# A bidirectional RWKV-7 layer on one core: a new issue order for the chunked delta rule, with work moved between VectorE, GpSimd and ScalarE

## The chip, the cores and the metric

The kernel runs on one core of a Trainium2 chip. The metric is the time of one execution on the device, in microseconds. The kernel before was timed in three runs. A profile was taken of one execution; its span is the time from the first to the last instruction.

The core has five engines that run side by side, each working through its own list of instructions in the order in which the program issued them: TensorE (PE, matrix products; PEld is its loading of weights), VectorE (DVE), ScalarE (ACT), GpSimd (POOL) and SyncE (SP), which here does nothing but start DMA transfers. An instruction that has to wait for another engine or for a transfer holds up all that stands behind it on its own engine.

## The reference

One layer is computed for two sequences, 4096 and 512 tokens of width 1024: RMS norm, an input projection of which most columns are mixed with their neighbours in time, 16 heads of a delta rule with 64 x 64 states that is run forward and backward in time, a group norm, a gate, an output projection, a residual add and a final RMS norm. The part that matters here is the recurrence:

```python
def step(s, inp):
    r_t, w_t, k_t, v_t, kk_t, a_t = inp
    sa = jnp.einsum("bhvk,bhk->bhv", s, -kk_t)
    s = (s * w_t[:, :, None, :]
         + sa[..., None] * (kk_t * a_t)[:, :, None, :]
         + v_t[..., None] * k_t[:, :, None, :])
    return s, jnp.einsum("bhvk,bhk->bhv", s, r_t)
...
y_fwd = delta_rule_scan(r_h, heads(decay[:, :, 0]), heads(k_dir[:, :, 0]), v_h, kk, heads(a[:, :, 0]))
y_bwd = flip(delta_rule_scan(flip(r_h), flip(heads(decay[:, :, 1])), ...))
y = y_fwd + y_bwd
```

The decay and the mixing rate `a` of each token come from small products of rank 64 with a tanh and a sigmoid.

## The kernel before

There are three phases. The first does the norm and the input projection and leaves `r`, `k`, `v`, the normed keys and the gates in DRAM. The third does the group norm, the gate and the output projection. The change touches only the second, which does the recurrence.

**Tiling.** The second phase works on 72 blocks: 4 groups of four heads times 18 stretches of 256 tokens, 16 of them of the long sequence and 2 of the short one. A block D does both directions d (0 forward, 1 backward) and two halves hf (two heads each), and each half has four chunks i of 64 tokens. In a chunk the recurrence is replaced by products of 64 x 64 matrices, for which a unit triangular matrix is inverted for every head, direction and chunk.

**The operations of a block.** Each has a short name in the table `ISSUE`; where it ends in digits these are the half and the chunk (or part).
- SyncE: `lt`, `lk`, `lb`, `lr` load the low-rank activations, `k`, the normed keys and `r` (`load_ta` L549, `load` L541); `uv` loads `v` (L780). `ga` writes the diagonal 32 x 32 parts of the masked scores to DRAM (`gather`, L712), `gb` and `gw` read them back as `lt` and `w`, one matrix per partition (L723, L731). `S1` and `S2` write the inverse out to DRAM and read it back into `xt` (L751, L762). `yo` stores the output.
- `stage_a` (L556): `lw`, `la` are products on TensorE; `tw`, `tW`, `ta`, `tA`, `pl`, `e1`, `e2`, `fc`, `fC` are on ScalarE; `sn` (a running sum), `bf`, `bF`, `al`, `aL`, `kf`, `kF`, `rh`, `rH`, `en`, `kb`, `kk`, `kK` are on VectorE. Then `s0` to `s7` are products of scores on TensorE, `m0` to `m3` mask them on VectorE into `sc`, `x0` and `x1` transpose on TensorE, `c0` and `c1` copy on ScalarE.
- `elim` (L739): `E0` to `E14` are 15 parts of two elimination steps each on GpSimd. A step is a product into `tm` and an add into `w`, each of which needs the one before. Ones are then set on the diagonal, at the head of `S1`.
- `stage_b` (L790): `xr` transposes the pulled-in inverse on VectorE; `g0`, `g1`, `h0`, `h1` are products on TensorE and `gc`, `gC`, `hc`, `hC` copies on ScalarE that fill in the 64 x 64 inverse.
- `chain` (L841), for each half and chunk, in the order in which the data flow: `a` and `r` (TensorE, into one PSUM tile), `q` (ScalarE, copy to `rs`), `u` (TensorE, product with the inverse), `v`, `V` (ScalarE, copy to `uv`), `z` (TensorE, the new part of the state), `w`, `W` (VectorE, into the state `sn`), which the next chunk's `r` needs. `p` and `P` (`decay`, L869) write the decayed old state for direction 0 (on VectorE) and direction 1 (on ScalarE). `y` (TensorE) and `Y`, `Z` (ScalarE) give the output.

**What sets the order.** The order is written out by hand. Operation n of block D gets the position D * PERIOD + ISSUE[n], with PERIOD 27.706; all operations of all blocks are sorted by it and issued in that order (L530). Positions have no unit and don't say when an operation runs; only the order counts. Since a block's positions go from -2.9 to 146.6, five or six blocks are under way at a time. For an operation of block D at position v, v modulo 27.706 is its place in the period and v divided by 27.706 is how many blocks it lags.

**Buffers.** `k2` and `uv` have two and three buffers, `kb`, `r2`, `ta` and the tile of `bk` one, `lt` and `w` two; `xt` is one of two fixed tiles. A PSUM tile `px` is shared by `x`, `g` and `h`, another (`pl`) by the low-rank products. `BURST` adds some products at the beginning and in the last three blocks that keep TensorE busy; it isn't changed.

Of the kernel before, what the change touches and what calls it, by code (L numbers as in the profile page):

```python
# [23 lines left out]
ISSUE = {  # L24
# [44 lines left out]
def kernel(  # L69
# [62 lines left out]
    with ExitStack() as p1:  # L132
# [98 lines left out]
        # slots: one product of a column tile with a third of a token block. Each slot has small products  # L231
        # (put amid the large one) and work of the other engines, both queued by the slots before.
# [233 lines left out]
    with ExitStack() as p2:  # L466
# [89 lines left out]
        def stage_a(D, hf):  # L556
# [3 lines left out]

            def lora(x):
                z = ps.tile([128, 2, 256], F32, tag="pl", name="z")
                E["z", x] = z
                for d in range(2):
                    for n, w in enumerate(wa_q[D // NQ]):
                        PE.matmul(z[:, d, :], w[:, d, x, hf, :], S["ta"][:, d, x, :], start=(n == 0), stop=(n == 1))  # L566

            def tanh(x, d):
                n = ("qw", "qa")[x]
                if d == 0:  # L570
                    E[n] = epool.tile([128, 2, 256], F32, tag=n, name=n)
                q = E[n][:, 0, :] if d == 0 else E[n][:, 1, ::-1]
                ACT.activation(q, E["z", x][:, d, :], AF.Tanh, scale=(0.5, -0.5)[x], bias=(w0v, a0v)[x][d][:, p:p + 1])  # L573
# [29 lines left out]
            def alpha(d):  # L603
                if d == 0:
                    S["ar", hf] = d3.tile([128, 2, 4, 128], F32, tag="ar", name="ar")
                    S["tb", hf] = d3.tile([128, 2, 4, 128], F32, tag="tb", name="tb")
                    S["sc", hf] = d3.tile([128, 2, 2, 4, 128], F32, tag="sc", name="sc")
                k2 = S["k2", hf].rearrange("p d (i t) -> p d i t", t=64)
                stt(S["ar", hf][:, d, :, 0:64], k2[:, 0] if d == 0 else k2[:, 1, ::-1, ::-1], kkv[:, p:p + 1],
# [6 lines left out]
            def rho(d):  # L616
                r2 = S["r2", hf].rearrange("p d (i t) -> p d i t", t=64)
                pp = E["pp"]
                if d == 0:
                    tt(DVE, S["ar", hf][:, 0, :, 64:128], r2[:, 0], pp[:, 0, :, 1:65])  # L620
                else:
                    tt(DVE, S["ar", hf][:, 1, :, 64:128], r2[:, 1, ::-1, :], pp[:, 1, :, 64:0:-1])

            def ends():
                S["pt", hf] = d3.tile([128, 2, 4], F32, tag="pt", name="pt")
                DVE.tensor_copy(out=S["pt", hf], in_=E["pp"][:, :, :, 64])
# [8 lines left out]
            def kap_k(d):  # L635
                bk = E["bk"]
# [29 lines left out]
            def tcopy(d):  # L666
                ACT.activation(S["tb", hf][:, d], E["tp", d], AF.Copy)
# [71 lines left out]
        def elim(D):  # L739
            S = st[D]  # L740

            def e_step(j):
                lt, w = S["lt"], S["w"]
                m, n = (j + 1) // 2, 31 - j
                tm = bpool.tile([128, 128], F32, tag="tm", name="tm")
                tm = tm[:, 0:m * n].rearrange("p (c t) -> p c t", t=n)
                sh = [128, m, n]
                tt(POOL, tm, lt[:, j - 1, j + 1:32].unsqueeze(1).to_broadcast(sh), w[:, 0:m, j:j + 1].to_broadcast(sh))
                tt(POOL, w[:, 0:m, j + 1:32], w[:, 0:m, j + 1:32], tm, ALU.add)

            def scatter1():  # L751
                w = S["w"]
                wf = w.rearrange("p a b -> p (a b)")
                for c in range(2):
                    POOL.memset(wf[64 * c:64 * c + 64, c:c + 511:34], 1.0)
# [323 lines left out]
```

## Time and profile before

| | |
|---|---|
| runs | 4937.08, 4940.35, 4935.35 us; median 4937.08 |
| span of the profiled execution | 4926.0 us |
| median less span, what lies around the span | 11.1 us |
| mean granted clock of TensorE | 0.952 |
| busy in the span | PE 4484.3, DVE 3474.9, ACT 2726.9, POOL 2711.4 us |

The profiled execution's own time is listed by the page as its span only; a whole execution of the same program is some 11 us longer, as the third row shows. The page names lines of the kernel as L797 and so on. Operations that go through a small helper carry the helper's line: L86 is a product or sum of two tensors, on VectorE or GpSimd, L89 is VectorE's operation with a scalar per partition. In a timeline a row gives start, duration, engine, line, operation, output and input with their shapes, and in brackets how long the engine had been idle before and what ended it. In a row of waits stand the total, how often, and the longest. In a row of stages stand the stretch, its length, the busy time with the number of instructions of PE, PEld, DVE, ACT and POOL, the granted clock, the share of the DMA engines and GB/s.

### The profile page before, as it was taken

The page shows a single profiled execution, that of the slowest core. Times are in us where ns is not written, and L with a number is a line of the kernel's source. Part 1 is how long each engine was busy: PE and PEld are TensorE (multiplying, and loading weights), DVE is VectorE, ACT ScalarE, POOL GpSimd, SP SyncE. Part 2 cuts the span into 40 slices and gives each one's busy share as a digit, 9 for nine tenths or more (in the row PEclk, how much of TensorE's full clock was granted, in tenths as well). Part 3 has the DMA queues.
Part 4 walks back from the last instruction along what each step waited for, and adds up shares of the span by engine and source line. Part 5 has one row for each costly group of instructions (what it writes and reads, how often), then busy time and mean ns, then how long its engine had stood idle before and what let it go on. Part 6 is the DMA issues. An engine that isn't in the chain of part 4 may idle for free. (4 is left out here: it accounts for less than half of the span.)

```text
span 4926.0 us, 133131 instructions
## 1 busy us (share of the span) xinstructions
PE 4484.3 (91%) x51995; PEld 3943.8 (80%) x52005; DVE 3474.9 (71%) x6182; ACT 2726.9 (55%) x6779; POOL 2711.4 (55%) x5480
## 2 busy tenths in 40 slices
PE   8999999999999998688888888889899888896999
PEld 8999999999999997577677677677777777665887
DVE  5666666656664565677777777777777777756998
ACT  5544444444454444567666666667677666663322
POOL 3333333333333332677776777767777777764553
PEclk9999999999999998899999999989999899998999
DMA  4433333433433333455565555655656555547885
GB/s 135 147 112 112 106 113 113 123 94 122 127 106 105 97 105 109 124 141 142 134 153 142 138 142 140 150 139 140 149 142 151 137 143 140 144 98 240 269 269 188
DMA packets 1278855, 687.50 MB, mean 140 GB/s; under 512 B 665232, under 2 KB 1242768, under 8 KB 1278224
## 3 DMA queue, kind: packets, MB, share of 16 engines
q1 hardware_dynamic: 1278224, 678.99, 50.1%
q8 instruction: 408, 6.68, 0.6%
q14 instruction: 223, 1.83, 0.1%
HBM read 457.50 MB, written 221.25 MB: 138 GB/s over the span
## 5 line engine op out<-in xcount | busy, mean ns | idle before, releaser
L86 POOL TENSOR_TENSOR tm<-lt,w 128x30 f32<-128x30 f32 (+7 forms) x2160 | 864.7, 400 | 521.8 <-DMA w<-gd 340.8
L227 PE MATMUL acc<-hh,wh 128*128 128x384 f32 x3264 | 1108.0, 339 | 0.0
L229 PE MATMUL acc<-hh,wl 128*128 128x384 f32 x3264 | 1096.3, 336 | 0.0
L228 PE MATMUL acc<-hl,wh 128*128 128x384 f32 x3264 | 1096.2, 336 | 0.0
L86 POOL TENSOR_TENSOR w<-w,tm 128x30 f32<-128x30 f32 (+7 forms) x2160 | 893.5, 414 | 169.3
L228 PEld LDWEIGHTS acc<-hl,wh 128*128 128x128 f32 x3264 | 617.3, 189 | 0.0
L227 PEld LDWEIGHTS acc<-hh,wh 128*128 128x128 f32 x3264 | 617.0, 189 | 0.2
L229 PEld LDWEIGHTS acc<-hh,wl 128*128 128x128 f32 x3264 | 616.1, 189 | 0.0
L86 POOL TENSOR_TENSOR s<-u 128x384 f32<-128x384 f32 (+2 forms) x312 | 271.0, 868 | 602.1 <-ACT u L452 428.2
L89 DVE SCALAR_TENSOR_TENSOR sn<-pr,pt,sn 128x128 f32<-128x128 f32 x1152 | 346.5, 340 | 266.6 <-PE pr L894 233.8
L655 PE MATMUL sp<-ar,bk 64*128 64x128 f32 x4608 | 424.9, 309 | 9.3 <-DVE bk L86 7.4
L86 DVE TENSOR_TENSOR sc<-sp,mask 128x512 f32<-128x512 f32 x576 | 385.1, 679 | 12.7 <-PE sp L655 12.6
L452 ACT ACTIVATE u<-acc 128x384 f32<-128x384 f32 x408 | 198.2, 486 | 353.3 <-PE acc L229 353.1
L655 PEld LDWEIGHTS sp<-ar,bk 64*128 64x128 f32 x4608 | 321.7, 199 | 89.6 <-issue 32.7
L885 PE MATMUL pr<-rs,xt 64*64 64x64 f32 x4608 | 262.0, 233 | 90.6 <-ACT rs L867 89.1
L888 ACT ACTIVATE uv<-pr 64x128 f32<-64x128 f32 x1152 | 310.7, 270 | 41.9 <-PE pr L885 28.9
L86 POOL TENSOR_TENSOR xl<-rk,xh 128x384 fp32r<-128x384 f32 (+1 forms) x96 | 97.4, 1015 | 428.2 <-ACT xh L259 428.2
L867 ACT ACTIVATE rs<-py 128x128 f32<-128x128 f32 x576 | 159.2, 277 | 302.7 <-PE py L863 296.4
L885 PEld LDWEIGHTS pr<-rs,xt 64*64 64x64 f32 x4608 | 182.7, 136 | 163.0 <-ACT rs L867 110.9
L566 PE MATMUL z<-ta,wah 128*128 128x256 f32 x576 | 191.8, 352 | 115.1 <-ACT qw L573 95.5
L797 DVE STREAM_TRANSPOSE x<-xt 128x512 f32<-128x512 f32 x72 | 51.2, 711 | 338.4 <-DMA xt<-wd 338.4
L86 DVE TENSOR_TENSOR xl<-kq,xh 128x384 fp32r<-128x384 f32 (+1 forms) x96 | 93.3, 972 | 269.7 <-ACT xh L259 269.7
(163 smaller groups left out, 10470.7 us busy)
## 6 DMA issues: line engine op xcount, KB each, us to landing
wr<-in_rw_in_dram SPq DMA_DIRECT2D x136, 512.0 KB, 4.3
ta<-ta_d SPq DMA_DIRECT2D x144, 256.0 KB, 2.9
k<-k_d SPq DMA_DIRECT2D x288, 128.0 KB, 2.8
r<-r_d SPq DMA_DIRECT2D x288, 128.0 KB, 2.2
kb<-kb_d SPq DMA_DIRECT2D x288, 128.0 KB, 3.4
uv<-v_d SPq DMA_DIRECT2D x288, 128.0 KB, 2.9
y_d<-ys SPq DMA_DIRECT2D x144, 256.0 KB, 3.9
lt<-gd SPq DMA_DIRECT2D x144, 240.0 KB, 3.6
```

The source lines that it names most:

```text
L86: eng.tensor_tensor(out=out, in0=a, in1=b, op=op)
L89: DVE.scalar_tensor_tensor(out=out, in0=a, scalar=s, in1=b, op0=op0, op1=op1)
L227: PE.matmul(ps, wh[:, k, :], hh[:, k, :], start=(k == 0), stop=False)
L228: PE.matmul(ps, wh[:, k, :], hl[:, k, :], start=False, stop=False)
L229: PE.matmul(ps, wl[:, k, :], hh[:, k, :], start=False, stop=(k == KT - 1))
L452: ACT.activation(u[:, 2 + s * SUB:2 + (s + 1) * SUB], ps[:, 0:SUB], AF.Copy, scale=(0.5 if typ == "g" else 1.0))
L566: PE.matmul(z[:, d, :], w[:, d, x, hf, :], S["ta"][:, d, x, :], start=(n == 0), stop=(n == 1))
L655: PE.matmul(E["sp"][h][:, d, j, :], bk_(d, i)[hs], ar[hs, d, i, :], start=True, stop=True)
L797: DVE.transpose(out=x, in_=S["xt"][:, :, 0:32])
L867: ACT.activation(S["rs", hf], rp, AF.Copy)
L885: PE.matmul(up[ua[d], hs], S["xt"][ua[d], 8 * hf + 4 * h + i, :], rs[ua[d], hs], start=True, stop=True)
L888: ACT.activation(S["uv", hf][ua[d], d, (i, 3 - i)[d], :], up[ua[d]], AF.Copy)
```

## The change

Three things change, all in the second phase.

1. Every entry of `ISSUE` has a new value, so the order of all operations changes on all five engines. PERIOD stays.
2. `E6` and `E12`, the parts 6 and 12 of the fifteen of the elimination, run on VectorE, with a temporary tile of their own (`td`). The setting of the diagonal becomes an operation of its own (`ms`), still on GpSimd.
3. `p`, the decay of the forward state, runs on ScalarE for all four chunks (`ACT_DECAY = 4`).

The rest follows from the new order: tiles that were made by one named operation are made by whichever comes first (`kept`, `tile_bk`, `state_tile`), the PSUM tiles `iv` of `g` and `h` have names of their own, and the state before a chunk is looked up by its number (`before`).

```diff
+ON_DVE = (6, 12)
+ACT_DECAY = 4
 ISSUE = {
-    "wa": -2.946, "lt": 0.000, "lk0": 2.020, "lw0": 3.600, "lr0": 5.680, "tw0": 8.955, "tW0": 9.315,
...
-    "m01": 44.495, "m11": 45.105, "x01": 45.320, "c01": 45.960, "s41": 46.412, "s61": 46.854, "x11": 48.502,
-    "s51": 48.944, "c11": 49.142, "s71": 49.386, "m21": 50.626, "m31": 52.116, "ga1": 58.442, "gb": 62.192,
-    "gw": 64.482, "E0": 68.302, "E1": 69.594, "E2": 71.070, "E3": 72.701, "E4": 74.458, "E5": 76.312,
-    "E6": 78.234, "E7": 80.196, "E8": 82.169, "E9": 84.124, "E10": 86.032, "E11": 87.864, "E12": 89.592,
-    "E13": 91.187, "E14": 92.620, "S1": 95.488, "uv0": 98.678, "S2": 99.958, "xr": 103.358, "a00": 105.682,
...
+    "wa": -2.9000, "lt": 0.0000, "lk0": 1.1591, "lw0": 1.2805, "lb0": 3.3493, "tw0": 7.3949, "tW0": 8.8003,
...
+    "e11": 26.1877, "lr1": 27.5209, "s70": 27.6598, "s60": 27.6701, "rH1": 27.7889, "al1": 27.9700,
+    "s40": 28.0035, "s50": 28.7095, "bf1": 28.7498, "e21": 28.8191, "aL1": 29.0697, "fc1": 29.1549,
+    "rh1": 30.5646, "fC1": 33.6847, "kf1": 33.7227, "en1": 33.7493, "kb1": 34.0198, "kF1": 35.3220,
...
+    "s61": 41.9178, "s71": 42.8163, "c01": 42.8473, "s41": 43.6381, "m31": 43.6723, "ga0": 44.0974,
+    "m21": 44.6119, "ga1": 45.5600, "x11": 45.7879, "c11": 46.5981, "gw": 49.6933, "gb": 50.5948, "E0": 57.5603,
+    "E1": 62.9549, "E2": 64.2336, "E3": 68.6505, "E4": 70.0206, "E5": 70.3026, "E6": 73.5289, "E7": 74.7859,
+    "E8": 76.3981, "E9": 79.0079, "E10": 82.8529, "uv0": 83.5557, "E11": 83.7589, "E12": 84.4780,
+    "E13": 87.3066, "E14": 87.5877, "ms": 88.8890, "S1": 90.1739, "S2": 94.4958, "xr": 98.0045, "g0": 102.1712,
+    "g1": 102.6785, "uv1": 103.3862, "gC": 103.6546, "gc": 104.5328, "a00": 104.7541, "p00": 107.0296,
+    "r00": 107.9962, "h0": 108.9094, "q00": 109.5492, "P00": 109.7186, "h1": 109.9664, "a10": 110.5160,
+    "hC": 110.6414, "hc": 110.6737, "r10": 111.1384, "q10": 111.3443, "P10": 111.3638, "u00": 111.3691,
+    "u10": 111.3799, "v00": 111.3876, "V00": 111.5611, "v10": 111.5624, "a11": 111.6107, "V10": 111.6683,
+    "z00": 111.6767, "a01": 111.7563, "z10": 112.1606, "W00": 112.2069, "w00": 112.4946, "r01": 112.6950,
...
+    "W13": 136.3979, "Y11": 136.5489, "w13": 136.6701, "Z11": 137.9200, "yo": 142.4142,
 }
...
+            def kept(n, *shape):
+                if (n, hf) not in S:
+                    S[n, hf] = d3.tile([128, *shape], F32, tag=n, name=n)
+                return S[n, hf]
...
+            def tile_bk():
+                if "bk" not in E:
+                    E["bk"] = bpool.tile([128, 2, 576], F32, tag="bk", name="bk")
+                return E["bk"]
...
-            def e_step(j):
+            def e_step(j, eng):
                 lt, w = S["lt"], S["w"]
                 m, n = (j + 1) // 2, 31 - j
-                tm = bpool.tile([128, 128], F32, tag="tm", name="tm")
+                n_ = "tm" if eng is POOL else "td"
+                tm = bpool.tile([128, 128], F32, tag=n_, name=n_)
                 tm = tm[:, 0:m * n].rearrange("p (c t) -> p c t", t=n)
                 sh = [128, m, n]
-                tt(POOL, tm, lt[:, j - 1, j + 1:32].unsqueeze(1).to_broadcast(sh), w[:, 0:m, j:j + 1].to_broadcast(sh))
-                tt(POOL, w[:, 0:m, j + 1:32], w[:, 0:m, j + 1:32], tm, ALU.add)
+                tt(eng, tm, lt[:, j - 1, j + 1:32].unsqueeze(1).to_broadcast(sh), w[:, 0:m, j:j + 1].to_broadcast(sh))
+                tt(eng, w[:, 0:m, j + 1:32], w[:, 0:m, j + 1:32], tm, ALU.add)
+
+            def ones():
+                wf = S["w"].rearrange("p a b -> p (a b)")
+                for c in range(2):
+                    POOL.memset(wf[64 * c:64 * c + 64, c:c + 511:34], 1.0)
...
             def e_block(b):
                 for j in range(1 + 30 * b // EB, 1 + 30 * (b + 1) // EB):
-                    e_step(j)
+                    e_step(j, DVE if b in ON_DVE else POOL)
...
+        def state_tile(hf, n):
+            if (hf, n) not in cur:
+                cur[hf, n] = spool.tile([128, 2, 128], F32, tag=f"sn{hf}", name="sn")
+            return cur[hf, n]
...
-            def first(i):
-                return i == 0 and q in FIRST
+            def before(i):
+                return zero if i == 0 and q in FIRST else cur[hf, 4 * D + i - 1]
...
             def decay(i, d):
...
+                pt, o = S["pt", hf][:, d, i:i + 1], state_tile(hf, 4 * D + i)[:, d, :]
+                if d == 0 and i >= ACT_DECAY:
+                    DVE.tensor_scalar(out=o, in0=before(i)[:, d, :], scalar1=pt, scalar2=None, op0=ALU.mult)
                 else:
-                    ACT.activation(o, cur[hf][:, d, :], AF.Copy, scale=pt)
+                    ACT.activation(o, before(i)[:, d, :], AF.Copy, scale=pt)
```

The places in the period of a few more operations that the prediction speaks of, in the new order: on TensorE r10 0.3, u00 0.5, u10 0.6, a11 0.8, z00 0.9, u01 2.8, a02 4.2, r11 5.0, z01 5.8, u11 6.1; on SyncE lt 0.0, uv0 0.4, lk0 1.2, lb0 3.3, yo 3.9, S1 7.1, S2 11.4, ga0 16.4, lk1 17.1, ga1 17.9, lr0 18.6, lb1 20.2, uv1 20.3, gw 22.0, gb 22.9, lr1 27.5. SyncE's order before was lt 0.0, lr1 1.0, lk0 2.0, ga1 3.0, lr0 5.7, gb 6.8, yo 8.1, gw 9.1, lb0 10.3, lk1 11.4, S1 12.4, ga0 13.7, uv0 15.6, S2 16.8, lb1 19.0, uv1 25.7.

More of the change, by code (lines that the diff above doesn't have):

```diff
@@ L569, in tanh @@
                 n = ("qw", "qa")[x]
-                if d == 0:
+                if n not in E:
                     E[n] = epool.tile([128, 2, 256], F32, tag=n, name=n)
@@ L594, in bfac @@
             def bfac(d):
-                if d == 0:
+                if "ah" not in E:
                     E["ah"] = epool.tile([128, 2, 256], F32, tag="qw", name="ah")
@@ L619, in rho @@
                 if d == 0:
-                    tt(DVE, S["ar", hf][:, 0, :, 64:128], r2[:, 0], pp[:, 0, :, 1:65])
+                    tt(DVE, kept("ar", 2, 4, 128)[:, 0, :, 64:128], r2[:, 0], pp[:, 0, :, 1:65])
                 else:
-                    tt(DVE, S["ar", hf][:, 1, :, 64:128], r2[:, 1, ::-1, :], pp[:, 1, :, 64:0:-1])
+                    tt(DVE, kept("ar", 2, 4, 128)[:, 1, :, 64:128], r2[:, 1, ::-1, :], pp[:, 1, :, 64:0:-1])
             def ends():
-                S["pt", hf] = d3.tile([128, 2, 4], F32, tag="pt", name="pt")
-                DVE.tensor_copy(out=S["pt", hf], in_=E["pp"][:, :, :, 64])
+                DVE.tensor_copy(out=kept("pt", 2, 4), in_=E["pp"][:, :, :, 64])
+            def tile_bk():
+                if "bk" not in E:
+                    E["bk"] = bpool.tile([128, 2, 576], F32, tag="bk", name="bk")
+                return E["bk"]
             def kap_b():
-                bk = bpool.tile([128, 2, 576], F32, tag="bk", name="bk")
-                E["bk"] = bk
+                bk = tile_bk()
                 e8 = E["ee"]
@@ L635, in kap_k @@
             def kap_k(d):
-                bk = E["bk"]
+                bk = tile_bk()
                 e8 = E["ee"]
@@ L650, in scores @@
                 ar, i = S["ar", hf], 2 * i2 + j
-                if (d, j) == (0, 0):
-                    E["sp"] = [ps.tile([128, 2, 2, 128], F32, tag=("pa", "pb")[h], name="sp") for h in range(2)]
+                if ("sp", i2) not in E:
+                    E["sp", i2] = [ps.tile([128, 2, 2, 128], F32, tag=("pa", "pb")[h], name="sp") for h in range(2)]
                 for h in range(2):
                     hs = slice(64 * h, 64 * h + 64)
-                    PE.matmul(E["sp"][h][:, d, j, :], bk_(d, i)[hs], ar[hs, d, i, :], start=True, stop=True)
+                    PE.matmul(E["sp", i2][h][:, d, j, :], bk_(d, i)[hs], ar[hs, d, i, :], start=True, stop=True)
             def masks(i2, h):
-                tt(DVE, S["sc", hf][:, :, h, 2 * i2:2 * i2 + 2, :], E["sp"][h],
+                tt(DVE, kept("sc", 2, 2, 4, 128)[:, :, h, 2 * i2:2 * i2 + 2, :], E["sp", i2][h],
                    mask.unsqueeze(2).to_broadcast([128, 2, 2, 128]))
@@ L666, in tcopy @@
             def tcopy(d):
-                ACT.activation(S["tb", hf][:, d], E["tp", d], AF.Copy)
+                ACT.activation(kept("tb", 2, 4, 128)[:, d], E["tp", d], AF.Copy)
             for n, *f in (
@@ L713, in gather @@
             S = st[D]
-            if f == 0:
+            if "gd" not in S:
                 S["gd"] = dsc.tile([2, 2, 2, 4, 2, 32, 32], F32, tag="gd", name="gd")
@@ L772, in e_block @@
                 for j in range(1 + 30 * b // EB, 1 + 30 * (b + 1) // EB):
-                    e_step(j)
+                    e_step(j, DVE if b in ON_DVE else POOL)
             for b in range(EB):
                 add(f"E{b}", D, e_block, b)
+            add("ms", D, ones)
             add("S1", D, scatter1)
@@ L799, in g_mm @@
             def g_mm(n):
-                if n == 0:
-                    S["iv"] = ps.tile([128, 16, 32], F32, tag="px", name="iv2")
-                pt = S["iv"]
+                if "iv2" not in S:
+                    S["iv2"] = ps.tile([128, 16, 32], F32, tag="px", name="iv2")
+                pt = S["iv2"]
                 for x in range(8 * n, 8 * n + 8):
@@ L810, in g_cp @@
                 q = 64 * d
-                ACT.activation(S["g"][q + 32:q + 64], S["iv"][q + 32:q + 64], AF.Copy)
+                ACT.activation(S["g"][q + 32:q + 64], S["iv2"][q + 32:q + 64], AF.Copy)
             def x_mm(n):
-                if n == 0:
-                    S["iv"] = ps.tile([128, 16, 32], F32, tag="px", name="iv3")
-                pt = S["iv"]
+                if "iv3" not in S:
+                    S["iv3"] = ps.tile([128, 16, 32], F32, tag="px", name="iv3")
+                pt = S["iv3"]
                 for x in range(8 * n, 8 * n + 8):
@@ L824, in x_cp @@
                 q = 64 * d
-                ACT.activation(S["xt"][q:q + 32, :, 32:64], S["iv"][q:q + 32], AF.Copy)
+                ACT.activation(S["xt"][q:q + 32, :, 32:64], S["iv3"][q:q + 32], AF.Copy)
             for n, *f in (
@@ L858, in step_r @@
             def step_r(i):
-                if first(i):
-                    cur[hf] = zero
-                S["old", hf, i] = cur[hf]
                 for d in range(2):
-                    PE.matmul(rp[ua[d], :], S["ar", hf][:, d, i, 0:64], cur[hf][:, d, :], start=False, stop=True)
+                    PE.matmul(rp[ua[d], :], S["ar", hf][:, d, i, 0:64], before(i)[:, d, :], start=False, stop=True)
             def copy_r(i):
@@ L869, in decay @@
             def decay(i, d):
-                if d == 0:
-                    S["sn", hf] = spool.tile([128, 2, 128], F32, tag=f"sn{hf}", name="sn")
-                if first(i):
-                    cur[hf] = zero
-                pt, o = S["pt", hf][:, d, i:i + 1], S["sn", hf][:, d, :]
-                if d == 0:
-                    DVE.tensor_scalar(out=o, in0=cur[hf][:, d, :], scalar1=pt, scalar2=None, op0=ALU.mult)
+                pt, o = S["pt", hf][:, d, i:i + 1], state_tile(hf, 4 * D + i)[:, d, :]
+                if d == 0 and i >= ACT_DECAY:
+                    DVE.tensor_scalar(out=o, in0=before(i)[:, d, :], scalar1=pt, scalar2=None, op0=ALU.mult)
                 else:
-                    ACT.activation(o, cur[hf][:, d, :], AF.Copy, scale=pt)
+                    ACT.activation(o, before(i)[:, d, :], AF.Copy, scale=pt)
             def step_u(i):
@@ L905, in step_y @@
                 for d in range(2):
-                    PE.matmul(o[d], S["ar", hf][:, d, i, 64:128], S["old", hf, i][:, d, :], start=True, stop=False)
+                    PE.matmul(o[d], S["ar", hf][:, d, i, 64:128], before(i)[:, d, :], start=True, stop=False)
                 for h in range(2):
```

13 lines of the change are left out of this document (2 added, 11 removed), and 51 rows, old and new, of the table ISSUE.

## The prediction

> **What bounds the kernel now.** Only the second phase is touched, so I first ask where it lies and how long one block of it takes. The page gives the span, the view of one tile's instructions gives the first and last VectorE transpose of the pulled-in inverse (one per block, 72 blocks), and the view by stages gives the engines' busy time between those two.
>
> ```profile
> span 4926.0 us, 133131 instructions
> L797 DVE STREAM_TRANSPOSE x<-xt x72: 711/711/714, 2036.5 to 4416.0; 128x512 f32<-128x512 f32 x72
> 2036.50:4416.00 2379.50, 2104.46 (x38417) 1689.79 (x38425) 1755.48 (x4113) 1612.02 (x4625) 1738.26 (x4381) 0.93 0.57 141
> ```
>
> 71 periods take 2379.5 us, so one block costs 33.5 us. Per block TensorE is busy 29.6 us, VectorE 24.7, ScalarE 22.7, GpSimd 24.5 (the columns are PE, weight loads, DVE, ACT, POOL). TensorE is idle 3.9 us per block, and a granted clock of 0.93 means that it ran at half speed for some 0.14 of the time, 4.7 us per block. No engine is full. So I next read who waits for whom in the same stretch (total, times, longest).
>
> ```profile
> DVE x L797 <- DMA xt<-wd: 333.2, 71, 16.4
> POOL tm L86 <- DMA w<-gd: 286.6, 65, 8.9
> ACT qw L573 <- DVE bk L86: 203.1, 66, 17.5
> PE pr L885 <- ACT rs L867: 87.4, 90, 1.3
> PE z L566 <- ACT qw L573: 80.7, 64, 1.7
> PE iv L806 <- DVE x L797: 56.5, 52, 2.2
> PE pr L894 <- ACT uv L888: 21.7, 72, 0.7
> ```
>
> VectorE stands 4.7 us in every block for the inverse to come back from DRAM, and GpSimd stands 4.0 us for the next block's matrices. Each engine works strictly in the issued order, so VectorE's stand holds up what is queued behind it: ScalarE's `qw` waits for `bk`, and TensorE waits for `qw` and `x`, (80.7 + 56.5) / 71 = 1.9 us of its 3.9 us. The rows of four microseconds show the hole and its echo (last figures: clock, DMA share, GB/s).
>
> ```profile
> 3020.00:3024.00 4.00, 3.24 (x50) 2.54 (x46) 0.31 (x1) 2.48 (x8) 3.31 (x9) 1.00 0.71 154
> 3024.00:3028.00 4.00, 2.28 (x67) 2.18 (x68) 4.00 (x9) 1.56 (x4) 3.45 (x8) 0.64 0.38 113
> 3028.00:3032.00 4.00, 4.00 (x33) 2.88 (x34) 3.96 (x9) 0.83 (x3) 3.37 (x9) 0.51 0.51 157
> ```
>
> VectorE does 0.31 us of work in 3020 to 3024, TensorE thins out, and then the granted clock is 0.64 and 0.51.
>
> Why do both stands occur in every block? The timelines of VectorE, SyncE's queue and GpSimd give the ring.
>
> ```profile
> 3023.69 0.71 DVE L797 STREAM_TRANSPOSE x<-xt 128x512 f32<-128x512 f32 x1 [4.94 <-DMA xt<-wd]
> 3027.75 0.68 DVE L86 TENSOR_TENSOR sc<-sp,mask 128x512 f32<-128x512 f32 x1
> ```
> ```profile
> 3014.43 1.26 SPq L760 DMA_DIRECT2D wd<-w  x2
> 3020.18 2.14 SPq L768 DMA_DIRECT2D xt<-wd  x4
> 3032.00 2.33 SPq L720 DMA_DIRECT2D gd<-sc  x4
> 3039.46 0.81 SPq L546 DMA_DIRECT2D r<-r_d  x2
> 3043.19 1.64 SPq L737 DMA_DIRECT2D w<-gd  x2
> ```
> ```profile
> 3004.79 0.49 POOL L86 TENSOR_TENSOR w<-w,tm 128x84 f32<-128x84 f32 x1
> 3007.11 0.61 POOL L86 TENSOR_TENSOR tm<-lt,w 128x56 f32<-128x56 f32 x1
> 3010.23 0.30 POOL L755 MEMSET w<- 64x16 f32 x2
> 3014.42 0.24 POOL L86 TENSOR_TENSOR tm<-lt,w 128x30 f32<-128x30 f32 x1 [3.90 <-DMA w<-gd]
> 3027.14 0.41 POOL L86 TENSOR_TENSOR tm<-lt,w 128x128 f32<-128x128 f32 x1
> ```
>
> Block D's elimination starts at 3014.42 and ends, memsets included, one period after 3010.53, at 3044.0: 29.6 us. Its transpose follows 13.2 us after the memsets (3010.53 to 3023.69). Behind the transpose stand masks of block D+2, done at 3028.43, 4.7 us after its start. Only then may D+2's gather go out, but SyncE issues it at 3032.00 to 3034.33 (5.9 us), then waits with a load of `r` until 3039.46, and is done with `w<-gd` at 3044.83 (10.5 us). The elimination of D+2 begins 3.1 us later, at 3014.42 + 67.0 - 33.5 = 3047.9. The pieces, 29.6 + 13.2 + 4.7 + 5.9 + 10.5 + 3.1 = 67.0 us, are exactly two periods of 33.5. This **ring over two blocks** sets the pace; TensorE does not.
>
> **The change, part by part.**
>
> *Two parts of the elimination move to VectorE.* Part 6 is the steps of 126 and 119 elements, part 12 those of 78 and 65, two instructions each: eight instructions per block. GpSimd loses 1.8 us of part 6 (from the 126 row below, 0.472 + 0.523, to the start of part 7 at 3027.14) plus the stretch from 3005.28 to 3007.11 for part 12, about 3.9 us in all. On VectorE no such instruction was run; the floor is its 8-element copy (0.300), the ceiling GpSimd's own 0.523. I take 0.33, nearest the 128-element `sn` rows: 8 x 0.33 = 2.6 us, bounds 2.4 to 4.2.
>
> ```profile
> L86 POOL TENSOR_TENSOR w<-w,tm 128x126 f32<-128x126 f32 x142 | 74.2, 523 | 11.1
> L86 POOL TENSOR_TENSOR tm<-lt,w 128x126 f32<-128x126 f32 x142 | 67.0, 472 | 11.1
> L626 DVE COPY pt<-pp 128x8 f32<-128x8 f32 x138 | 41.4, 300 | 0.0
> L876 DVE TENSOR_SCALAR sn<-sn,pt 128x128 f32<-128x128 f32 x551 | 179.2, 336 | 3.1 <-PE py L906 2.9
> L878 ACT ACTIVATE sn<-sn,pt 128x128 f32<-128x128 f32 x551 | 219.0, 398 | 1.8
> ```
>
> *The forward decay* is eight instructions per block: VectorE loses 8 x 0.336 = 2.7 us and ScalarE gains 8 x 0.398 = 3.2 us. VectorE stays at 24.7 - 2.7 + 2.6 = 24.6 us and ScalarE comes to 25.9. Both stay below what TensorE needs (next part), but ScalarE's copies are on the recurrent path of the states and now meet more company.
>
> *The queue of SyncE.* Nothing is added to it; its order changes. S1 (to `wd`) now has S2 (to `xt`) right behind it, with no loads between, and ga0, lk1, ga1, lr0, lb1, uv1, gw, gb follow. So S2 makes the queue wait for S1's landing; queued behind are the gathers, and they would wait for the masks behind the transpose anyway. I price the two hops with the landings of the page's kind of row:
>
> ```profile
> wd<-w SPq DMA_DIRECT2D x142, 128.0 KB, 2.8
> xt<-wd SPq DMA_DIRECT2D x284, 64.0 KB, 2.6
> ```
>
> S1's second issue starts 0.6 us in and lands 2.8 us later, at 3.4; S2's last of four starts 1.6 us on and lands at 3.4 + 1.6 + 2.6 = 7.6 us, in place of 13.2. The three loads now between ga1 and gw (some 0.8 to 1.3 us each by the `r` and `wd` rows) hide ga1's landing, and the wait for `r`'s buffer is gone from there: `lr0` stands at 18.64, its buffer's last readers (`rH1`, `rh1`) at 27.79 and 30.56, a period earlier relative to it.
>
> *The ring after the change.* Taking positions modulo the period of 27.706, a period reads: E0 of the next block on GpSimd at 2.1, E13, E14 and memsets from 4.2, S1 7.1, S2 11.4, transpose 14.9, last masks 16.0 and 16.9 (of the block two later), E6 on VectorE 18.1, E7 on GpSimd 19.4 through E11, E12 on VectorE at 1.4. That makes a ring of **one** period: E6 on VectorE 1.4; E7 to E11 11.6 (3027.14 to 3005.28, one period on); E12 with two engine changes 1.5, beside which E0 of the next block runs (four instructions of the size in the row of 3014.42, some 1.3 us); E13 to memsets 3.4 (3007.11 to 3010.53); hops 7.6; transpose and two masks 0.7 + 0.68 + 0.6 = 2.0. The sum is 27.5 us. The gather's ring closes over one period too, from E0 through memsets, hops, masks, ga1 (2.3), three loads (3.0), gw and gb (2.8) and a landing (3.1): 1.3 + 3.4 + 7.6 + 2.0 + 2.3 + 3.0 + 2.8 + 3.1 = 25.5 us. Both are shorter than TensorE's need, but not by much.
>
> [...]
>
> *TensorE's need.* Its work is unchanged. In the half-clock stretch one `r` product group takes 0.69 us, at full clock 0.44:
>
> ```profile
> 3007.02 0.44 PE L863 MATMUL py<-sn,ar 128*64 128x128 f32 x4
> 3030.12 0.69 PE L863 MATMUL py<-sn,ar 128*64 128x128 f32 x4
> ```
>
> So of 4.7 us at half clock 4.7 x (1 - 0.44 / 0.69) = 1.7 us was loss, and the work at full clock is 29.6 - 1.7 = **27.9 us**. To that come three things. First, the new order has places where a result cannot be back in time. The rows below give the round trips: r at 3007.02, its copy at 3007.60; copy at 3013.29, u at 3013.62; so r to u takes 0.91 us, of which r's own turn is 0.37. u at 3004.04, copies at 3004.67, z at 3005.29: 1.25 us, less u's turn of 0.38.
>
> ```profile
> 3007.60 0.28 ACT L867 ACTIVATE rs<-py 128x128 f32<-128x128 f32 x1 [0.45 <-PE py L863]
> 3013.29 0.28 ACT L867 ACTIVATE rs<-py 128x128 f32<-128x128 f32 x1
> ```
> ```profile
> 3004.04 0.45 PE L885 MATMUL pr<-rs,xt 64*64 64x64 f32 x8
> 3005.29 0.45 PE L894 MATMUL pr<-uv,tb 128*64 128x64 f32 x8
> 3013.62 0.45 PE L885 MATMUL pr<-rs,xt 64*64 64x64 f32 x8 [1.03 <-ACT rs L867]
> ```
>
> So an r wants 0.54 us of other products behind it before its u, and a u 0.87 before its z. Between r10 and u10 stands only u00 (0.38), between r11 and u11 only z01 (0.38); u01 has a02 and r11 (0.71) and u00 has u10 and a11 (0.76) before their z. These four are short by 0.16 + 0.16 + 0.16 + 0.11 = 0.6 us; the old order had every such pair covered. Second, queueing on ScalarE: today TensorE waits (87.4 + 21.7) / 71 = 1.5 us per block for copies; I scale it by ScalarE's load, 25.9 / 31 against 22.7 / 33.5, to 1.9 us. Third, some clock loss stays: I take half, 0.8 us, because the largest hole closes and small ones remain. [...]
>
> *Sum.* 27.9 + 0.6 + 1.9 + 0.8 = 31.2 us per block, 2.3 less: 71 x 2.3 = 163 us. Lead-in and tail: the first transpose moves from position 103.4 to 98.0 and the end from 43.2 behind it to 44.4, a net of 4.2 positions at 33.5 / 27.7 = 1.2 us, 5 us less. The span would be 4926 - 168 = 4758 us. The runs' median, 4937, lies 11 us above the span; I keep that, and get **4769 us**.
>
> **The rivals.** (A) *TensorE nearly full*: clock loss gone and queueing only half of today's: 27.9 + 0.6 + 0.7 = 29.2 us, which gives 4937 - 71 x 4.3 - 5 = 4627 us. For it speaks that the rings have 27.5 us; against it ScalarE's longer queue. (B) *The one-period ring becomes the pace, slower than before.* Place: VectorE at E6 and E12, where it now stands for GpSimd, with the states' updates queued behind. If the two hops still take 13.2 us (the DMA engines are already busy 0.57 of the stretch, and the new order sends its transfers in one long row), the ring is 27.5 + 5.6 = 33.1; if VectorE also comes to E6 and E12 with about one scan-sized backlog in all (1.3 us, my estimate of its queue there), 34.4 us: 4937 + 71 x 0.9 - 5 = 4996 us. It decides from a ring above 33.5, that is 6 us more than the sum above. For it: four changes of engine and two hops in one period; against it: S2 no longer has SyncE's other work ahead. (C) *The gain is eaten by short waits*: TensorE's idle time stays 3.9 us and the clock 0.93 though the stands are gone, 33.5 us per block, 4932 us. Against it: 1.9 of the 3.9 us are pinned on the stand. (D) Half of the gain only, 32.4 us: 4937 - 78 - 5 = 4854 us, if the missing cover and ScalarE's growth, which I put at 0.6 + 0.4, cost 2.2 us, as they would if each copy came a tenth of a microsecond later than today.
>
> **How the numbers follow.** Forecast 0.55, A 0.11, D 0.17, B 0.12, C 0.05. A measurement of this kernel can tell about 0.2%, 10 us, from no change. Forecast, A and D are faster: 0.83. C is the middle of no change and just faster: 0.04 for the same. B is slower: 0.13 with C's edge. The forecast's own range is 30.2 to 32.2 us per block, 4698 to 4840. The range reaches over D and most of C, and towards A to 29.7 us: 4660 to 4932, leaving out B, and the better half of A.
>
> **What would show it.** Right: the spacing of the transposes falls to about 31.2 us; the waits of VectorE for `xt` and of GpSimd for `w` fall well below 1 us per block; S1's issue to the transpose takes under 9 us; granted clock above 0.95; ScalarE's waits for TensorE shrink while TensorE's for `rs` grow. Wrong: new waits of VectorE's `td` and `w` for GpSimd, or of GpSimd's `tm` for VectorE above some 3 us per block (B); a clock still at 0.93 (C).

## The result and the profile after

The changed kernel ran in 4771.35 us (median, 4767.1 to 4778.97) beside 4936.22 us for the kernel before on the same chip: a ratio of 0.9667 with a 95% interval of 0.9653 to 0.9681. The forecast was 4769 us.

The same three rows as before the change, from the page, the view of the transpose's tile and the view by stages:

```profile
span 4772.0 us, 133366 instructions
...
L810 DVE STREAM_TRANSPOSE x<-xt x72: 697/699/714, 2028.0 to 4258.4; 128x512 f32<-128x512 f32 x72
...
2028.00:4258.40 2230.40, 1983.10 (x38351) 1580.65 (x38351) 1717.81 (x4114) 1745.80 (x5181) 1640.56 (x3818) 0.96 0.62 150
```

A block now takes 2230.4 / 71 = 31.4 us in place of 33.5. The second phase between first and last transpose gave 149.1 us, lead-in and tail (span less that stretch) 4.9 us: 2546.5 before, 2541.6 after. TensorE is idle (2230.4 - 1983.1) / 71 = 3.5 us per block, busy 27.9, and its mean clock is 0.96.

Who waits for whom in that stretch. The row of the transpose among VectorE's groups stands in for its wait (busy, mean, idle before and what ended it); the others are totals, times and longest.

```profile
L810 DVE STREAM_TRANSPOSE x<-xt 128x512 f32<-128x512 f32 x71 | 49.7, 700 | 2.1 <-DMA xt<-wd 2.1
```
```profile
POOL tm L91 <- DVE w L91: 288.2, 139, 7.4
ACT rs L882 <- PE py L878: 154.2, 175, 2.9
DVE ar L91 <- DMA r<-r_d: 123.5, 54, 5.8
PE py L915 <- ACT rs L882: 99.2, 212, 0.7
PE pr L896 <- ACT rs L882: 47.0, 70, 0.8
PE pr L905 <- ACT uv L899: 33.8, 129, 0.6
PE z L576 <- DMA ta<-ta_d: 28.1, 46, 3.8
POOL tm L91 <- DMA lt<-gd: 15.3, 19, 2.4
```

The two stands that the prediction built on are gone: VectorE's wait for `xt` fell from 333.2 us to 2.1, GpSimd's wait for the gathered matrices from 286.6 (for `w`) to 15.3 (for `lt`). New are GpSimd's waits for VectorE's two parts, 4.1 us per block, VectorE's wait for the load of `r`, 1.7, and TensorE's wait at the output product (L915) for a copy of `rs`, 1.4.

The timelines of SyncE, GpSimd and VectorE show the way round:

```profile
3004.74 1.26 SPq L772 DMA_DIRECT2D wd<-w  x2
3007.99 1.93 SPq L780 DMA_DIRECT2D xt<-wd  x4
...
3015.32 1.80 SPq L729 DMA_DIRECT2D gd<-sc  x4
...
3021.55 1.27 SPq L746 DMA_DIRECT2D w<-gd  x2
```
```profile
3004.59 0.30 POOL L764 MEMSET w<- 64x16 f32 x2
...
3016.59 0.89 POOL L91 TENSOR_TENSOR tm<-lt,w 128x128 f32<-128x128 f32 x1 [1.84 <-DVE w L91]
```
```profile
3013.42 0.70 DVE L810 STREAM_TRANSPOSE x<-xt 128x512 f32<-128x512 f32 x1
3014.05 1.25 DVE L91 TENSOR_TENSOR sc<-sp,mask 128x512 f32<-128x512 f32 x2
3015.22 0.26 DVE L91 TENSOR_TENSOR td<-lt,w 128x126 f32<-128x126 f32 x1
```

From the memsets' end at 3004.89 to the transpose are 8.5 us in place of 13.2, and the transpose doesn't wait. The gather goes out at 3015.32, as the masks end at 3015.30; before, 3.6 us passed there. `w<-gd` follows it 6.2 us later (before 11.2).

### The profile page after: what moved, and what is told of

Same layout as the page of the kernel before. It is cut to its first block, busy times and chain, and to the rows that moved or that the text cites. A ratio compares the mean times of both kernels' runs of the same rounds, so it can differ in the third digit from the quotient of the medians.

```text
span 4772.0 us, 133366 instructions
## 1 busy us (share of the span) xinstructions
PE 4369.3 (92%) x52005; PEld 3842.4 (81%) x52005; DVE 3437.4 (72%) x6182; ACT 2866.8 (60%) x7355; POOL 2608.6 (55%) x4904
## 4 chain that ended last, share of the span: by engine, by line
PE 63%; ACT 14%; DVE 7%; DMA 6%; issue 5%; POOL 2%; SPq 1%; ACTq 0%; DVEq 0%; POOLq 0%
PE acc L232 10%; PE acc L234 10%; PE acc L233 10%; PE acc L1039 8%; DMA ta<-ta_d 4%; ACT uv L899 3%; PE z L576 3%; PE py L915 3%; PE pr L896 3%; PE sp L664 3%; PE py L919 2%; PE py L878 2%; PE pr L905 2%; PE tp L673 2%; DMA r<-r_d 2%
## 5 line engine op out<-in xcount | busy, mean ns | idle before, releaser
L91 POOL TENSOR_TENSOR tm<-lt,w 128x120 f32<-128x120 f32 (+7 forms) x1872 | 818.6, 437 | 486.8 <-DVE w L91 291.1
L91 POOL TENSOR_TENSOR w<-w,tm 128x120 f32<-128x120 f32 (+7 forms) x1872 | 838.3, 448 | 146.7
L889 ACT ACTIVATE sn<-sn,pt 128x128 f32<-128x128 f32 x1120 | 436.5, 397 | 40.5 <-PE py L915 34.4
L91 DVE TENSOR_TENSOR sc<-sp,mask 128x512 f32<-128x512 f32 x576 | 372.3, 676 | 41.6 <-PE sp L664 40.7
L664 PE MATMUL sp<-ar,bk 64*128 64x128 f32 x4608 | 384.2, 296 | 8.2 <-DVE sc L91 6.4
L664 PEld LDWEIGHTS sp<-ar,bk 64*128 64x128 f32 x4608 | 302.5, 192 | 61.5 <-issue 30.6
L915 PE MATMUL py<-sn,ar 128*64 128x128 f32 x2240 | 250.6, 304 | 97.5 <-ACT rs L882 97.5
L896 PE MATMUL pr<-rs,xt 64*64 64x64 f32 x4608 | 251.3, 235 | 48.6 <-ACT rs L882 48.6
L905 PE MATMUL pr<-uv,tb 128*64 128x64 f32 x4608 | 260.1, 236 | 35.9 <-ACT uv L899 35.7
L91 DVE TENSOR_TENSOR wl<-wr,wh 128x1024 fp32r<-128x1024 f32 x136 | 182.8, 1344 | 137.0 <-ACT wh L223 136.8
```

The costliest lines, as they stand in the source:

```text
L91: eng.tensor_tensor(out=out, in0=a, in1=b, op=op)
L664: PE.matmul(E["sp", i2][h][:, d, j, :], bk_(d, i)[hs], ar[hs, d, i, :], start=True, stop=True)
L889: ACT.activation(o, before(i)[:, d, :], AF.Copy, scale=pt)
L896: PE.matmul(up[ua[d], hs], S["xt"][ua[d], 8 * hf + 4 * h + i, :], rs[ua[d], hs], start=True, stop=True)
L905: PE.matmul(zp[hs, d, hs], S["tb", hf][:, d, i, hs], S["uv", hf][:, d, (i, 3 - i)[d], hs], start=True, stop=True)
L915: PE.matmul(o[d], S["ar", hf][:, d, i, 64:128], before(i)[:, d, :], start=True, stop=False)
```

## The experiments

Each kernel was timed beside the kernel before on the same chip. Its median was 4940, 4961 and 4956 us in the three groups of runs, so the ratios are compared, not the times.

**The moves alone, in the old order.** The changed kernel's code with the old table:

```diff
-    "wa": -2.9000, "lt": 0.0000, "lk0": 1.1591, "lw0": 1.2805, "lb0": 3.3493, "tw0": 7.3949, "tW0": 8.8003,
...
+    "wa": -2.946, "lt": 0.000, "lk0": 2.020, "lw0": 3.600, "lr0": 5.680, "tw0": 8.955, "tW0": 9.315,
...
+    "E13": 91.187, "E14": 92.620, "ms": 95.487, "S1": 95.488, "uv0": 98.678, "S2": 99.958, "xr": 103.358, "a00": 105.682,
```

> The old order of all operations, with parts 6 and 12 of the elimination on VectorE and the forward decay on ScalarE (ms directly ahead of S1). Theory R (the ring over two blocks, closed by SyncE's order, sets the pace): the moves alone take 3.9 us off GpSimd in the ring and put about 2.2 us of VectorE back into it, with E6 right behind the transpose; 33 to 34.5 us per block, 4890 to 5000 us, VectorE still waits over 3 us per block for xt. Rival M (the gain is GpSimd's and VectorE's relieved load): below 4850 us.

Measured: 5004.77 us, ratio 1.0132 (1.01 to 1.0165). The waits of its second phase:

```profile
POOL tm L89 <- DVE w L89: 431.0, 142, 9.1
...
DVE x L808 <- DMA xt<-wd: 246.7, 67, 6.3
POOL tm L89 <- DMA w<-gd: 229.7, 63, 5.2
```

The old stands shrank to 3.5 and 3.2 us per block, and GpSimd got a third: 6.1 us per block for VectorE. In the old order the moves cost time. The time came out just above the range of theory R, and VectorE's wait for `xt` fits it; rival M, that the moves by themselves bring the gain, has fallen.

**The new order alone.**

```diff
-ON_DVE = (6, 12)
-ACT_DECAY = 4
+ON_DVE = ()
+ACT_DECAY = 0
```

> The new order of all operations, but all fifteen parts on GpSimd and the forward decay on VectorE as before. Theory R: most of the gain is there without the moves, 4740 to 4840 us; GpSimd then has 29.4 us of work per block, just below TensorE's pace. Rival M: above 4880 us.

Measured: 4816.93 us, ratio 0.9755 (0.9725 to 0.9785). That lies in the range of theory R: most of the gain, 2.4 of 3.3%, needs neither move.

**SyncE's queue alone, first try.** The order of the four other engines is the old one, and neither move is made; of the table, the entries that differ from the kernel before:

```diff
-    "lr0": 5.680, "lb0": 10.350, "lk1": 11.360, "ga1": 58.442, "gb": 62.192, "gw": 64.482, "S2": 99.958,
+    "lr0": 16.9, "lb0": 12.70, "lk1": 12.75, "ga1": 52.20, "gb": 54.60, "gw": 54.55, "S2": 95.60,
```

> The old order of TensorE, ScalarE, VectorE and GpSimd and no moves; in SyncE's queue alone seven operations stand elsewhere: S2 right behind S1, lb0 and lk1 behind S2, lr0 behind uv0, ga1 right behind the masks m31, gw and gb right behind uv1. Theory R: the hops fall from 13.2 to about 7.6 us and the gather's way from 16 to about 8, the ring falls below TensorE's need, VectorE's wait for xt goes below 1 us per block, 31.3 to 32.5 us per block, 4780 to 4865 us. Rival O (it is the order on the working engines that counts): above 4890 us.

Measured: 5256.5 us, ratio 1.0648 (1.0619 to 1.0676): a miss by more than 390 us. VectorE's wait for `xt` is no longer among the long ones, but these are, in the second phase:

```profile
DVE ar L89 <- DMA r<-r_d: 345.7, 68, 7.0
PE z L574 <- DMA ta<-ta_d: 331.2, 69, 6.8
POOL tm L89 <- DMA lt<-gd: 309.2, 35, 12.5
```
```profile
SPq L937 <- ACT ys L923: 450.6, 70, 11.6
SPq L727 <- DVE bk L89: 381.6, 66, 8.4
```

SyncE stood 5.4 us per block before a gather (L727), and the loads of `ta` and `r`, which I had left behind `ga1`, came late: TensorE waited 4.7 us per block for `ta`, VectorE 4.9 for `r`. The run doesn't decide between the theories, because it removed one wait and made others; it shows how much a queue's order alone can cost.

**SyncE's queue alone, second try.** Six entries, the loads of `ta` and of the second half's `r` staying ahead of `gw` and `gb`:

```diff
-    "lr0": 5.680, "ga1": 58.442, "gb": 62.192, "gw": 64.482, "S2": 99.958, "uv1": 108.818,
+    "lr0": 16.9, "ga1": 52.20, "gb": 56.52, "gw": 56.51, "S2": 95.60, "uv1": 107.568,
```

> Once more the old order with SyncE's queue alone changed, now without delaying the loads that are needed soon: S2 right behind S1; lr0 behind S2 and uv0; ga1 right behind the masks m31 with uv1 ahead of it; gw and gb behind ta's and r's loads. Theory R (the two-block ring set the pace): the hops fall from 13.2 to about 7.6 us, the way from m31 to the landing of w and lt from 19.5 to about 10, the ring to about 52 us for two blocks; VectorE's wait for xt goes below 1 us per block and the period to 31.3 to 32.8 us: 4780 to 4890 us. Rival O (the order on the working engines makes the gain; the ring was only one of several equally long): the waits go, but others take their place, 33 us or more per block, above 4900 us.

Measured: 4812.12 us, ratio 0.9696 (0.9663 to 0.9728). Tile, stage and waits:

```profile
L808 DVE STREAM_TRANSPOSE x<-xt x72: 697/699/712, 2033.7 to 4293.4; 128x512 f32<-128x512 f32 x72
...
2033.70:4293.40 2259.70, 2087.58 (x38363) 1679.06 (x38369) 1717.70 (x4113) 1602.64 (x4615) 1798.43 (x4386) 0.94 0.61 148
```
```profile
POOL tm L89 <- DMA lt<-gd: 91.1, 35, 9.5
...
DVE x L808 <- DMA xt<-wd: 13.3, 6, 10.9
```

31.8 us per block; the wait for `xt` went from 333.2 us to 13.3. Six entries in the queue of an engine that computes nothing give 3.0 of the 3.3% of the whole change, and the two intervals overlap. So the order of SyncE's queue set the pace, and rival O has fallen. Which of the six entries counts was not separated. Nor has any run the changed kernel's code with the old table and without the moves, so the rest of that code (tile names, `ms`) is counted with the six.

**The same with the forward decay on ScalarE** (`ACT_DECAY = 4` added to that table).

> The old order with SyncE's six entries moved (that alone 0.970) and the forward decay on ScalarE. If the decay's gain is a matter of VectorE's load: 0.955 to 0.963. If it depends on the new order, which puts the decays elsewhere on ScalarE: 0.968 to 0.980.

Measured: 4782.43 us, ratio 0.9637 (0.9596 to 0.9678), between the two expectations, and its interval overlaps that of the queue alone. It can't be told from the whole change, though all engines but SyncE run by the old table. Without the decay the new order gave 0.9755 and the old one with six entries 0.9696; with the decay (the new order's run is the second of the next two) they gave 0.9663 and 0.9637. No run shows a gain that the new order of the four working engines brings by itself.

**The decay and the two parts, each alone in the new order.** First the decay back on VectorE (`ACT_DECAY = 0`), the parts staying:

> The changed kernel with the forward decay back on VectorE; parts 6 and 12 stay on VectorE. VectorE gains 2.7 us per block, ScalarE loses 3.2. If the moves' 46 us (the order alone ran 4817) come from GpSimd's relief: 4760 to 4790 us. If they come from the decay, which leaves VectorE free for the states' updates: 4805 to 4840 us.

Measured: 4866.57 us, ratio 0.9809 (0.9778 to 0.9841). Then the parts back on GpSimd (`ON_DVE = ()`), the decay staying on ScalarE:

> The new order with the forward decay on ScalarE, but all fifteen parts of the elimination on GpSimd. Order alone ran at 0.9755 of before, order with the two parts at 0.981, the changed kernel at 0.967. If the decay's effect (0.986) doesn't depend on the parts: 0.959 to 0.965, faster than the changed kernel, and the two parts on VectorE cost time. If the parts pay only once VectorE is relieved of the decay: 0.970 or more.

Measured: 4787.71 us, ratio 0.9663 (0.9637 to 0.9688). So the decay is worth 0.9% without the parts (0.9755 to 0.9663) and 1.4% with them (0.9809 to 0.9667). The two parts on VectorE bring nothing once the decay is gone from it (0.9663 against 0.9667), and 0.9755 against 0.9809, with intervals that just touch, suggests that they cost something while it is there. What the decay gains shows mostly in the clock. The stretch 2036 to 4200 of the kernel with the parts and without the decay:

```profile
2036.00:4200.00 2164.00, 1909.25 (x35638) 1522.13 (x35631) 1757.87 (x4398) 1505.66 (x4322) 1481.14 (x3548) 0.92 0.61 147
```

Its transposes are 32.7 us apart, so TensorE is idle 3.9 us per block (3.5 with the decay moved) and busy 28.9 (27.9), and the clock is 0.92 in place of 0.96, which by the correction used below accounts for the 1 us of busy time. Why the clock is lower with the decay on VectorE was not traced.

**Three output products earlier.** The cause of TensorE's wait at L915 is seen in one place of the changed kernel (TensorE's and ScalarE's timelines):

```profile
3002.30 0.39 PE L878 MATMUL py<-sn,ar 128*64 128x128 f32 x4
...
3003.13 0.44 PE L915 MATMUL py<-sn,ar 128*64 128x128 f32 x4 [0.44 <-ACT rs L882]
```
```profile
3002.80 0.28 ACT L882 ACTIVATE rs<-py 128x128 f32<-128x128 f32 x1 [0.97 <-PE py L878]
```

An output product y follows an r of the same half at once and waits until ScalarE has copied that r. Both write the tile `py` in PSUM, the memory into which this kernel's products go, in different columns. It occurs 212 times, three per block: y00 behind r01, y01 behind r02, y12 behind r13. The edit moves the three y ahead of the product `a` that opens the next sum in that tile, and two of these `a` move too:

```diff
-    "y00": 113.5131, "y01": 119.3339, "a02": 115.0080, "y12": 131.8283, "a13": 129.0234,
+    "y00": 111.70, "y01": 116.64, "a02": 116.65, "y12": 129.42, "a13": 129.43,
```

> The changed kernel, with three output products moved ahead of the next chunk's first products: y00 ahead of a01, y01 and then a02 right behind z01, y12 and then a13 right behind z12. In the changed kernel these three stand directly behind r01, r02 and r13 in the same PSUM bank and TensorE waits 1.4 us per block there for the copy of r. If that wait lies on the path, 0.5 to 1.3 us per block go: 4680 to 4735 us. If another wait takes its place: 4760 to 4785 us.

Measured: 4716.69 us, ratio 0.9554 (0.9529 to 0.9579), faster than both kernels.

```profile
2029.40:4204.00 2174.60, 1941.89 (x38366) 1558.99 (x38364) 1754.54 (x4114) 1746.65 (x5182) 1572.31 (x3817) 0.98 0.64 154
```
```profile
PE pr L896 <- ACT rs L882: 113.6, 218, 0.8
```

30.6 us per block, 0.8 less. TensorE's waits for `rs` at L915, 99.2 us before the edit, are below the 6.5 us of the last row of the list, but TensorE's idle time fell only from 3.5 to 3.3 us: its wait for `rs` before u rose from 47.0 us to 113.6. The rest came from busy time, 27.9 to 27.4 us, with the clock at 0.98. So the time lies in the range that was expected if the wait was on the path, but by the correction used below 0.5 of the 0.8 us came by the clock, and only 0.2 by idle time.

**The load of r earlier.** One entry of the changed kernel:

```diff
-    "lr1": 27.5209,
+    "lr1": 21.80,
```

> The changed kernel with one entry changed: lr1, the load of r for the second half, stands ahead of gw in SyncE's queue instead of behind gb. In the changed kernel VectorE waits 1.7 us per block for it, most of it in some fifty blocks. If that wait is on the path, most of it goes: 4660 to 4730 us. If delaying gw and gb by about 1 us for it costs the elimination as much, or TensorE has other waits by then: 4755 to 4790 us.

Measured: 4886.07 us, ratio 0.9841 (0.9811 to 0.9871): a miss on both expectations. The waits of the second phase, SyncE's first:

```profile
SPq L729 <- DVE td L91: 241.4, 68, 7.9
...
SPq L551 <- DVE ar L91: 31.2, 45, 1.2
```
```profile
POOL tm L91 <- DMA lt<-gd: 77.2, 45, 4.5
PE z L576 <- DMA ta<-ta_d: 74.9, 95, 4.9
```

SyncE now waits for VectorE's last use of the one buffer of `r` (L551) with `gw`, `gb` and `ta` behind it. GpSimd's wait for `lt` rose from 15.3 us to 77.2 and TensorE's for `ta` from 28.1 to 74.9. The new wait is only 0.4 us per block, the block takes 1.3 us longer (32.7), and SyncE's stand before a gather (L729) grew more than any of these, from 150.8 us to 241.4; the whole way from the one to the other was not traced. A second buffer for `r`, which no run has, would test the wait itself, so whether VectorE's 1.7 us lie on the path isn't settled.

**Both edits together.**

> Both small edits of the order together: three output products ahead of the next chunk's first products (alone 4717 us) and lr1 ahead of gw. If they are independent: 4620 to 4690 us; if they close the same gap: 4700 to 4720 us.

Measured: 4891.35 us, ratio 0.9849 (0.9817 to 0.9882). That can't be told from the load alone (0.9841): beside it the output products bring nothing.

**Output products earlier and no parts on VectorE**, then **with part 12 only**.

> The kernel of the run before, with the three output products and two first products moved as in the run that gave 0.955. If all effects multiply: 0.945 to 0.953. If GpSimd's full 29.4 us per block now bounds: 0.955 to 0.965, with GpSimd's idle time below 1 us per block.

> The changed kernel with the five entries moved as in the run that gave 0.955, and only part 12 on VectorE, part 6 back on GpSimd. GpSimd waits for VectorE after both parts, 4.1 us per block in the changed kernel. If the wait after part 6, behind the transpose and the masks, is what costs: 0.945 to 0.952. If GpSimd's idle time is slack: 0.953 to 0.960.

Measured: 4709.41 us, ratio 0.9502 (0.9476 to 0.9527), and 4750.71 us, ratio 0.9591 (0.956 to 0.9622). The first is the fastest kernel of the study and lies in the range for effects that multiply; its interval just clears that of the same order with both parts (0.9554, 0.9529 to 0.9579). Part 12 alone can't be told from both, and is clearly slower than none: one part costs no less than two. The time lies in the range for slack in GpSimd's idle time, but then the step from no part to part 12 should cost nothing; neither account fits, and the cause stays open.

## Why the prediction was right, step by step

**The ring over two blocks: right in the queue that it named, which was tested by itself.** Six entries of SyncE's queue gave a ratio of 0.9696, and VectorE's wait for `xt` went with them. The sum of 67.0 us was no evidence, though. Its end, 3014.42 + 67.0 - 33.5, is set from the period itself, and any way from the start of one elimination to that of the next but one adds up to two periods, spare time included. What spoke for the ring were the waits at two of its links. At a third, the gather, 3.6 us passed after the masks were done at 3028.43, in which SyncE issued three loads (kernel before):

```profile
3028.55 0.89 SPq L554 DMA_DIRECT2D ta<-ta_d  x2
3030.05 0.81 SPq L546 DMA_DIRECT2D r<-r_d  x2
3031.16 0.80 SPq L546 DMA_DIRECT2D k<-k_d  x2
```

The data were there and the queue's order made the gather late; that is what the six entries changed. In the changed kernel the hops came to 8.5 us, where I had priced 7.6, and the transpose no longer waits, so they had time to spare.

**The sum, 31.2 us per block, was right by two errors that cancel.** TensorE's work was put at 27.9 us at full clock. Of the 27.9 us busy now, a clock of 0.96 means 0.08 x 31.4 = 2.5 us at half speed (the two traces record no granted clock but 1.00 and 0.50; of the 2090 rows of one microsecond from 2040 on, 1938 of the changed kernel read 1.00 and 122 read 0.50), of which by the prediction's own ratio (1 - 0.44 / 0.69 = 0.36) 0.9 us were loss; so the work is 27.0, with the clock's rounding worth 0.1. The clock's loss was forecast at 0.8 and came out right. The idle time was forecast at 0.6 + 1.9 = 2.5 us and is 3.5. Its two terms were for the pairs r to u and u to z, and those cost only (47.0 + 33.8) / 71 = 1.1 us: scaling the queueing up with ScalarE's load was wrong, since ScalarE is busier now (1745.80 / 71 = 24.6 us per block, before 22.7) and TensorE waits less at these pairs than before (87.4 + 21.7). What I didn't see was the y behind the r in the same PSUM tile, 1.4 us, and `ta` landing late, 0.4. I had gone through the covers by the data and not by the tiles that products share. That the errors cancel to 0.2 us per block is luck.

**The two parts on VectorE: cheaper there than forecast, and of no use.** I took 0.33 us each with a floor of 0.300. Measured:

```profile
L91 DVE TENSOR_TENSOR w<-w,td 128x126 f32<-128x126 f32 x71 | 20.6, 291 | 2.4
L91 DVE TENSOR_TENSOR td<-lt,w 128x65 f32<-128x65 f32 x71 | 16.8, 237 | 2.4
```

The eight sum to about 2.1 us, below the floor of 2.4: the 8-element copy was no lower bound. Part 12 stands beside E0 in some blocks only. Of two blocks, the first does, the second doesn't (GpSimd had stopped at 3030.54):

```profile
3000.22 0.24 POOL L91 TENSOR_TENSOR w<-w,tm 128x30 f32<-128x30 f32 x1
```
```profile
3000.28 0.28 DVE L91 TENSOR_TENSOR w<-w,td 128x78 f32<-128x78 f32 x1
...
3031.00 0.24 DVE L91 TENSOR_TENSOR w<-w,td 128x78 f32<-128x78 f32 x1
```

Of the 288 instructions of part 12, the 89 that ran while GpSimd worked took 0.27 us in the mean, the other 199 took 0.23: 0.04 us longer, and not by the 0.24 us of one of GpSimd's instructions. GpSimd gained less than I took: I had 3.9 us per block off it, and its busy time fell by 1.4, from 24.5 to 23.1 (1640.56 / 71), because its other steps ran longer in the new order (its add of 120 elements 0.79 us in the mean, before 0.51, though only one of the 213 ran beside the scan of the last section). I had also read part 6 as 1.8 us where the timeline before has 2.4 (3024.72 to 3027.14). That the relief was worth nothing is measured (0.9663 against 0.9667), and fits GpSimd's 4.1 us per block of waiting for VectorE, which don't set the pace.

**The forward decay: mis-sized.** I counted it as no more than load moved off VectorE and onto ScalarE, with a small growth of queueing. It is worth 0.9 to 1.4%, against my slight loss. With the parts on VectorE 1 us per block of it shows in the clock, 0.92 to 0.96, and 0.4 us in idle time; how it gets there stays open.

**The rivals.** B named the right place and a wrong sign: I wrote that GpSimd's wait for VectorE above 3 us per block would show it; it is 4.1 us and the ring doesn't set the pace, since the transpose finds its data ready. C fell: the clock rose from 0.93 to 0.96, though TensorE's idle time, 3.5 us, stayed near its 3.9. D's 32.4 us were not reached either, but short waits did cost 1 us more than the sum had for them. A's 29.2 us per block was not reached, even at the fastest run (30.6).

**The outer parts.** Lead-in and tail gained 4.9 us, where 5 were forecast. That 11 us lie around a span was wrong: the profiled execution of the changed kernel took 4773.78 us for a span of 4772.0. The spans differ by 154 us, where the sum had 168, and the medians by 165: the profiled execution of before, some 4928 us by its span, had been quicker than all its runs in the table, and part of the closeness to 4769 us is owed to that.

## What to carry to other kernels

Where two engines each wait for a transfer once per block, follow the data through the queue that issues the transfers until the loop closes. That its pieces add up to a whole number of periods proves nothing, as those of any loop do; look in it for a transfer that goes out late by the queue's order while its data are there, and change that order by itself. Here it was most of the gain. Keep what blocks on a late event behind the loads that others need soon: one load placed too early in the queue cost 1.7% here, and the two tries with the old order, which differ only in that queue, lie nearly 10% apart. In a new order check covers by the tiles that products share as well as by the data.

## What the runs showed of the hardware that was not expected

What a product of TensorE took depended on what stood next to it. In the changed kernel a u and the a behind it run through each other:

```profile
3003.73 0.27 PE L896 MATMUL pr<-rs,xt 64*64 64x64 f32 x2
3003.76 0.27 PE L873 MATMUL py<-uv,sc 64*64 64x64 f32 x2
...
3004.13 0.44 PE L878 MATMUL py<-sn,ar 128*64 128x128 f32 x4
```

Both groups are done in 0.40 us, while a u alone takes 0.38 (3005.21 to 3005.59) and an a alone as much (3016.34 to 3016.72). The second phase of the changed kernel has three such pairs per block, that of before two, and so has the old order with six entries of the queue moved. Correcting for the clock as above, the new order's products take 27.0 us per block in the changed kernel, and 28.0 in the old order with six entries of the queue moved (29.4 busy, clock 0.94). One pair more explains some 0.4 us of that; the rest wasn't traced. It gains no time by it, because TensorE is idle 3.5 us per block in the changed kernel and 2.4 in the other.

An instruction on VectorE of 65 elements took 233 to 237 ns and one of 126 elements 270 to 291, below the 293 ns of an 8-element copy in the same kernel. So the size alone doesn't set the short ones; the copy differs in kind, and reads every 65th element, and no run separates the two.

GpSimd's steps ran longer beside VectorE's scan. In the changed kernel its product of 110 elements took 1.26 us in the mean where it ran beside a scan (49 times) and 0.40 elsewhere (163). Two of them, the first beside the scan:

```profile
3022.84 1.24 DVE L591 TENSOR_TENSOR_SCAN d<-smask,d 128x520 f32<-128x520 bf16 x1 [0.36 <-ACT d L586]
```
```profile
3022.86 1.41 POOL L91 TENSOR_TENSOR tm<-lt,w 128x110 f32<-128x110 f32 x1
...
3024.82 0.46 POOL L91 TENSOR_TENSOR tm<-lt,w 128x110 f32<-128x110 f32 x1
```

Between the first and the last transpose of the changed kernel each of the 137 scans has a step of GpSimd's of over 1 us beside it; before, 74 of 137 had one. The prediction had no term for this.
